# The modulation of layer 2, computed beside layer 1's attention and scan instead of beside its output join

## The chip, the cores and the metric

The kernel runs on one core of a Trainium2 chip. The metric is the device time of one execution in microseconds (us); the median of three runs is compared. The engines of the core run side by side, each through its own list of instructions in a fixed order: PE multiplies matrices, DVE (VectorE) and ACT (ScalarE) do elementwise work and reductions, POOL (GpSimd) does some elementwise work, and SP only issues DMA transfers. An instruction that waits for a semaphore holds up everything behind it on its engine.

## The reference

Two layers on 512 tokens of width 1024, in float32. Layer 1 has a sparse attention branch (8 heads, a top-128 selection of keys) and a state space branch (a chunked scan over 4 groups of heads). Their outputs are joined, projected and added to `x` under a gate. Layer 2 has a band attention, a gated delta rule and a retrieval of experts ("peer"). Both layers are modulated by a vector that depends only on a conditioning vector `c`, and not on any token:

```
mod  = silu(c)   @ ada_w + ada_b        # layer 1: shift, scale, gate     (3 x 1024)
x    = x + gate * (merged @ w_out)      # the gate is needed only here
mod2 = silu(c_2) @ w_ada + b_ada        # layer 2: six parts              (6 x 1024)
```

The last 1024 columns of `mod` and the 6144 of `mod2` are the subject here. Nothing that is computed in between depends on them, so they can be computed at any place before the output projection of layer 1.

## The kernel before

All weights are float32. A weight matrix comes in blocks of 128 x 1024 (512 KB). `wload` (line 50 on) loads a block into a tile `wr`, ACT rounds it to `wh` (L51) and DVE, or POOL in a few places, computes the rest `wl` (L52). `gemm_t` then does 24 matmuls with it (L72 to L74), three per 128 rows, into a PSUM tile `g`. The tiles `wr` form one ring of four buffers in the order of the program: block n+4 can be loaded only after the last reader of block n is done.

The modulation is made of 56 such blocks, 8 for layer 1's gate and 48 for layer 2. A block is loaded into the same ring `wr` (L856), and one DVE instruction (L857) multiplies it by `silu(c)` and sums each row into a column of `acc2`. PE has no part in it. Ahead of the blocks of each layer stand the load of `c` (also a buffer of the ring), a tanh on ACT (L851) and two DVE instructions (L852, L853). After every 8 blocks L860 adds the bias. `mod_rest` makes a list of these 56 steps, and `pump(n)` takes the next n of them at the place where it is called.

Layer 1 runs in this order: the projections and top-k rounds that prepare the attention, with 8 gemms (`ssd_pre`) beside them; 8 attention heads (`att1_head`, each with one gemm of `w_za` and four softmax steps of 128 to 512 keys, `soft`); then for each of four groups the scan (`ssd_scan`), a gate of four gemms (`ssd_z`, weights `w_zs`), and four gemms that prepare the next group (`ssd_x`, `w_x`); then the join `out1`, which reads the attention output (`oatt_d`) and the scan output (`y_d`) back from memory and runs 48 gemms (`w_g`, `w_ba`, `w_bs`, `w_o`).

A softmax step runs through four engines: PE scores (L534), DVE maximum (L545, L547), ACT exponential (L549), DVE reciprocal and scaling (L551, L552), PE transposes (L556), ACT copy, PE product with the values (L560). The order on each engine is set by a scheduler when the program is built: it places the instructions of several steps between each other by its own estimate of their times, but takes buffers of a ring strictly in the order of the program. So gemms of later heads and of `ssd_x` stand between the steps of an attention head on PE. In the kernel before, `mod_rest` is called at the top of `out1`, and the pumps stand among its gemms.

Of the kernel before, what the change touches and what calls it, by code (L numbers as in the profile page):

```python
# [26 lines left out]
class Kernel:  # L27
# [218 lines left out]
    def layer1(self, st0):  # L246
        tc, nc, I = self.tc, self.nc, self.i
        cp = self.cp
        with ExitStack() as st:
            hp = st.enter_context(tc.tile_pool(name="hp", bufs=1, side="right"))  # L250
            mod = cp.tile([P, 24], F32, tag="mod1", name="mod1")
            G1 = cp.tile([P, 8], F32, tag="G1", name="G1")
            hs = [(self.t(hp, [P, T], F32R, f"hh{k}"), self.t(hp, [P, T], F32R, f"hl{k}")) for k in range(8)]
            with ExitStack() as s0:
                p0 = s0.enter_context(tc.tile_pool(name="p0", bufs=1))
                sc = self.silu_c(p0, "c_b")
                acc = p0.tile([P, 16], F32, tag="acc", name="acc1")
                xs = []
                for k in range(8):
                    x = self.t(p0, [P, T], F32, f"x{k}")  # L260
                    nc.sync.dma_start(x, I["xT"][:, k, :])
                    xs.append(x)
                ab = self.load(p0, "ada_b", [P, 24])
                ng = self.load(p0, "norm_g", [P, 8])

                self.ws = []

                def pre(k):
                    if k in (1, 2, 4, 6):
                        k0 = 2 * len(self.ws)  # L270
                        self.ws.append(self.wload(I["w_idx"][:, k0:k0 + 2, :]))
                    self.mod_block(p0, sc, "ada_w", 8 + k, acc)
                    self.mod_block(p0, sc, "ada_w", k, acc)
                    nc.vector.tensor_add(mod[:, k:k + 1], acc[:, k:k + 1], ab[:, k:k + 1])
                    nc.vector.tensor_add(mod[:, 8 + k:9 + k], acc[:, 8 + k:9 + k], ab[:, 8 + k:9 + k])
                    nc.vector.scalar_tensor_tensor(G1[:, k:k + 1], mod[:, 8 + k:9 + k], 1.0, ng[:, k:k + 1],
                                                   op0=OP.add, op1=OP.mult)

                ss = []
                for k in range(8):  # L280
                    sq = self.t(p0, [P, T], F32, "nm_sq", 4)
                    nc.scalar.activation(sq, xs[k], AF.Square)
                    if k not in (0, 6):
                        nc.vector.tensor_add(sq, sq, sp)
                    if k in (5, 7):
                        ss.append(sq)
                    sp = sq
                self.norm_mod(p0, xs, hs, G1, mod[:, 0:8], ss, pre)
            self.mod1 = mod
            self.gate1 = mod[:, 16:24]  # L290
            self.oatt_d = self.dr.tile([8, P, T], F32, tag="oatt_d", name="oatt_d")
            self.y_d = self.dr.tile([16, P, T], F32, tag="y_d", name="y_d")
            with ExitStack() as s1:
                self.ap = s1.enter_context(tc.tile_pool(name="at", bufs=1, reuse_waits="tile"))
                self.sp = s1.enter_context(tc.tile_pool(name="sp", bufs=1, reuse_waits="tile"))
                with tc.tile_pool(name="ap0", bufs=1, side="right", reuse_waits="tile") as self.ap0:
                    self.att1_pre(hs)
                    self.ssd_pre(hs)
                    self.pump(99)
                self.gp = s1.enter_context(tc.tile_pool(name="gp", bufs=1, side="right", reuse_waits="tile"))  # L300
                for h in range(8):
                    self.att1_head(h, hs)
                xs = self.ssd_x(0, hs)
                for g in range(4):
                    y = self.ssd_scan(g, xs)
                    zz = self.ssd_z(g, hs)
                    if g < 3:
                        xs = self.ssd_x(g + 1, hs)
                    self.ssd_gate(g, y, zz)
            self.est = ExitStack()  # L310
            self.ep = self.est.enter_context(tc.tile_pool(name="ep", bufs=1, reuse_waits="tile"))
            with ExitStack() as s2:
                self.out1(s2, hs)
# [360 lines left out]
    def ssd_z(self, g, hs):  # L674

        nc = self.nc
        zs = []
        for b in range(4):
            z = self.gemm_t(self.i["w_zs"][4 * g + b], 8, hs)
            tz = self.t(self.sp, [P, T], F32, "cv_t", 2)  # L680
            nc.scalar.activation(tz, z, AF.Tanh, scale=0.5)
            zz = self.t(self.ap, [P, T], F32, f"qT{b}")
            nc.vector.scalar_tensor_tensor(zz, tz, 1.0, z, op0=OP.add, op1=OP.mult)
            zs.append(zz)
        return zs

    def ssd_scan(self, g, xs):
# [93 lines left out]
    def out1(self, st, hs):  # L781
        tc, nc, I = self.tc, self.nc, self.i
        op = st.enter_context(tc.tile_pool(name="op", bufs=1, reuse_waits="tile"))
        self.mod_rest(op)
        half = []
        ehalf = [self.t(self.ep, [P, 4, T], F32, f"e{j}") for j in range(2)]
        for m in range(8):
            x = ehalf[m // 4][:, m % 4]
            self.gate(m, hs, x)
            half.append(x)  # L790
            self.pump(1 if m else 0)

        def parts(dram, n, tag):
            res = []
            for b in range(n):
                raw = self.t(op, [P, T], F32, "o_raw", 2)
                nc.sync.dma_start(raw, dram[b])
                hi = self.t(op, [P, T], F32R, f"{tag}h{b}")
                lo = self.t(op, [P, T], F32R, f"{tag}l{b}")
                self.split(raw, hi, lo)  # L800
                res.append((hi, lo))
            return res

        oa = parts(self.oatt_d, 8, "p")
        for m in range(8):
            yp = self.gemm_t(I["w_ba"][m], 8, oa)
            nc.vector.scalar_tensor_tensor(half[m], half[m], 1.0, yp, op0=OP.add, op1=OP.mult)
            self.pump(2)
        ys = parts(self.y_d, 16, "ys")
        ms = []  # L810
        for m in range(8):
            mg = self.t(op, [P, T], F32, "o_mg", 2)
            self.gate(8 + m, hs, mg)
            yp = self.gemm_t(I["w_bs"][m], 16, ys)
            nc.vector.scalar_tensor_tensor(mg, mg, 1.0, yp, op0=OP.add, op1=OP.mult)
            nc.vector.tensor_add(mg, mg, half[m])
            self.pump(4)
            hi = self.t(op, [P, T], F32R, f"ph{m}")
            lo = self.t(op, [P, T], F32R, f"pl{m}")
            self.split(mg, hi, lo, scale=0.5)  # L820
            ms.append((hi, lo))
        self.x1_d = self.dr.tile([8, P, T], F32, tag="x1_d", name="x1_d")
        self.x1 = []
        ex = [self.t(self.ep, [P, 4, T], F32, f"e{j}") for j in range(2)]
        for m in range(8):
            x = self.t(op, [P, T], F32, "o_raw", 2)
            nc.sync.dma_start(x, I["xT"][:, m, :])
            ps = self.gemm_t(I["w_o"][m], 8, ms)
            y = ex[m // 4][:, m % 4]
            nc.vector.scalar_tensor_tensor(y, ps, self.gate1[:, m:m + 1], x, op0=OP.mult, op1=OP.add)  # L830
            nc.sync.dma_start(self.x1_d[m], y)
            self.x1.append(y)
            self.sq_add(op, "o_mg", y, m, 8)
# [965 lines left out]
```

## Time and profile before

| | us |
|---|---|
| median of 3 runs (2573.65 to 2576.68) | 2576.07 |
| the profiled execution | 2574.48 |
| its span, from the first to the last instruction | 2572.8 |
| the 8 heads: first score to the last store of `oatt_d` | 198.5 to 331 |
| scan groups | about 345 to 585 |
| join `out1` | about 585 to 850 |

The profile gives the busy time of each engine in a stretch, the groups of instructions, who waited for whom, and the instructions in order of time. PE's busy time is made of pipelined matmuls: a row of 0.39 us starts 0.23 us after the one before it, so the count of matmuls in a stretch says more than its busy time. The granted clock of PE is shown as a share of 2.4 GHz.

### The profile page before, as it was taken

What the parts mean: (1) busy time and instruction counts of PE and PEld (TensorE: products, weight loads), DVE (VectorE), ACT (ScalarE), POOL (GpSimd) and SP (SyncE); (2) the same over time, 40 slices, a digit from 0 to 9 for tenths busy, and PEclk for the clock granted to TensorE, in tenths of its full rate; (3) what the DMA queues carried; (4) which work ended last, traced back from release to release, by engine and by line L of the source; (5) the groups of instructions that cost most, each with busy time, mean ns of one, the idle gap of its engine ahead of it and who ended that gap; (6) DMA issues with size and microseconds to landing.
All of it is one profiled execution on the core that took longest, in us unless ns stands there. A gap on an engine that the chain in (4) does not pass through costs nothing. (4 is left out here: it accounts for less than half of the span.)

```text
span 2572.8 us, 34773 instructions
## 1 busy us (share of the span) xinstructions
PE 2451.5 (95%) x12577; PEld 2043.5 (79%) x12577; DVE 1867.7 (73%) x3618; ACT 1052.5 (41%) x1881; POOL 693.8 (27%) x522
## 2 busy tenths in 40 slices
PE   5999999999999999899998889999899999999999
PEld 4777777778788778776777888999888888888887
DVE  8895666667764673555426899999777878888877
ACT  4444466653322443344433433444433333333332
POOL 3240010110001112420204556211343334443431
PEclk8999999999999999999999999999999999999999
DMA  7222212228865311101422466799999999989995
GB/s 248 75 80 81 74 56 79 69 72 285 288 223 183 110 58 50 58 21 50 137 82 83 145 192 194 270 327 331 334 309 331 335 329 345 355 308 332 337 337 207
DMA packets 199596, 500.43 MB, mean 195 GB/s; under 512 B 20096, under 2 KB 85888, under 8 KB 196352
## 3 DMA queue, kind: packets, MB, share of 16 engines
q1 hardware_dynamic: 159104, 338.81, 39.7%
q0 software_dynamic: 36864, 134.23, 14.7%
q10 hardware_dynamic: 3456, 25.17, 2.4%
q8 instruction: 99, 1.62, 0.3%
q14 instruction: 73, 0.60, 0.1%
HBM read 448.01 MB, written 50.14 MB: 194 GB/s over the span
## 5 line engine op out<-in xcount | busy, mean ns | idle before, releaser
L51 ACT ACTIVATE wh<-wr 128x1024 fp32r<-128x1024 f32 (+2 forms) x424 | 442.6, 1046 | 622.8 <-PE g L73 337.1
L74 PE MATMUL g<-hh,wl 128*128 128x384 f32 (+1 forms) x1792 | 660.2, 368 | 23.8 <-POOL wl L52 20.5
L72 PE MATMUL g<-hh,wh 128*128 128x384 f32 (+1 forms) x1792 | 665.0, 371 | 15.5 <-ACT act L1639 10.0
L73 PE MATMUL g<-hl,wh 128*128 128x384 f32 (+1 forms) x1792 | 659.2, 368 | 0.0
L52 DVE TENSOR_TENSOR wl<-wr,wh 128x1024 fp32r<-128x1024 f32 (+3 forms) x362 | 440.4, 1217 | 189.7 <-ACT wh L51 187.3
L74 PEld LDWEIGHTS g<-hh,wl 128*128 128x128 f32 x1792 | 342.5, 191 | 61.6 <-POOL wl L52 23.5
L72 PEld LDWEIGHTS g<-hh,wh 128*128 128x128 f32 x1792 | 342.4, 191 | 52.8 <-ACT act L1639 10.8
L73 PEld LDWEIGHTS g<-hl,wh 128*128 128x128 f32 x1792 | 342.1, 191 | 38.8 <-issue 8.6
L73 PE MATMUL acc<-wl,gh 128*128 128x512 f32 x768 | 303.8, 396 | 0.0
L74 PE MATMUL acc<-wh,gl 128*128 128x512 f32 x768 | 303.7, 395 | 0.0
L72 PE MATMUL acc<-wh,gh 128*128 128x512 f32 x768 | 303.7, 395 | 0.0
L1676 POOL DMA_INDIRECT row<-in_rows_dn,idx x128 | 167.1, 1306 | 357.0 <-DVE row L1682 315.4
L1676 POOL DMA_INDIRECT row<-in_rows_up,idx x128 | 175.2, 1369 | 268.5 <-DVE gacc L1695 249.0
L52 POOL TENSOR_TENSOR wl<-wr,wh 128x1024 fp32r<-128x1024 f32 x62 | 152.5, 2468 | 239.5 <-ACT wh L51 230.6
L51 ACT ACTIVATE gh<-ga 128x384 fp32r<-128x384 f32 x128 | 67.2, 525 | 335.5 <-issue 193.7
L1682 DVE SCALAR_TENSOR_TENSOR row<-row,h2n 128x1024 f32<-128x1024 f32 x128 | 166.3, 1309 | 21.7 <-DMA row<-in_rows_dn,idx 21.7
L74 PEld LDWEIGHTS acc<-wh,gl 128*128 128x128 f32 x768 | 144.4, 188 | 34.7
L73 PEld LDWEIGHTS acc<-wl,gh 128*128 128x128 f32 x768 | 144.4, 188 | 34.4
L72 PEld LDWEIGHTS acc<-wh,gh 128*128 128x128 f32 x768 | 144.4, 188 | 34.4
L1695 DVE SCALAR_TENSOR_TENSOR gacc<-row,gw,gacc 128x1024 f32<-128x1024 f32 x127 | 162.6, 1280 | 11.8 <-DMA row<-in_rows_up,idx 10.8
L52 DVE TENSOR_TENSOR gl<-ga,gh 128x384 fp32r<-128x384 f32 x128 | 73.3, 572 | 58.7 <-ACT gh L51 50.3
L98 PE MATMUL g<-wh,hh 128*128 128x512 f32 (+3 forms) x256 | 96.1, 377 | 13.4 <-ACT hh L223 11.8
(553 smaller groups left out, 3851.9 us busy)
## 6 DMA issues: line engine op xcount, KB each, us to landing
wr<-in_w_dn SPq DMA_DIRECT2D x128, 512.0 KB
wr<-in_w_up SPq DMA_DIRECT2D x128, 512.0 KB
wr<-in_ada_w SPq DMA_DIRECT2D x56, 512.0 KB
g_d<-stage ACTq DMA_DIRECT2D x24, 1024.0 KB
gr<-g_d SPq DMA_DIRECT2D x32, 768.0 KB
wr<-in_w_x SPq DMA_DIRECT2D x24, 512.0 KB
act_d<-act SPq DMA_DIRECT2D x63, 192.0 KB
ar<-act_d SPq DMA_DIRECT2D x63, 192.0 KB
```

What stands on the lines that cost most here:

```text
L51: nc.scalar.activation(hi, src, AF.Copy)
L52: eng.tensor_sub(lo, src, hi.bitcast(F32))
L72: mm(ps, ah, bh, start=first, stop=False)
L73: mm(ps, ah, bl, start=False, stop=False)
L74: self.mm = mm(ps, al, bh, start=False, stop=last)
L98: mm(pss[t], hh[:, tt], wh[:, k], start=f, stop=False)
L1676: nc.gpsimd.indirect_dma_start(r, None, src, bass.IndirectOffsetOnAxis(ap=self.idx[:, s:s + 1], axis=0))
L1682: nc.vector.scalar_tensor_tensor(r, r, 1.0, self.h2n, op0=OP.mult, op1=OP.mult, accum_out=act[:, s:s + 1])
L1695: nc.vector.scalar_tensor_tensor(acc, r, w[:, s:s + 1], acc, op0=OP.mult, op1=OP.add)
```

## The change

The call of `mod_rest` moves from the top of `out1` to the place ahead of the loop over the attention heads. The tile for `silu(c)` and the biases move with it into the pool `gp`. The pumps in `out1` go. Instead, 4 blocks are taken after each head (32), and 1, 2, 1 and 2 blocks after the four gemms of each `ssd_z` (24): all 56. In the kernel before, 55 were taken in `out1` and one in the first stage of layer 2.

```
@@ layer1
                 self.gp = s1.enter_context(tc.tile_pool(name="gp", ...))
+                self.mod_rest(self.gp)
                 for h in range(8):
                     self.att1_head(h, hs)
+                    self.pump(4)
@@ ssd_z
             zs.append(zz)
+            self.pump(2 if b % 2 else 1)
@@ out1
         op = st.enter_context(tc.tile_pool(name="op", ...))
-        self.mod_rest(op)
...
             half.append(x)
-            self.pump(1 if m else 0)
...
             nc.vector.scalar_tensor_tensor(half[m], half[m], 1.0, yp, op0=OP.add, op1=OP.mult)
-            self.pump(2)
...
             nc.vector.tensor_add(mg, mg, half[m])
-            self.pump(4)
```

On SP, the list of transfers at the start of the heads was, before, the eight blocks of `w_za` one behind the other, and the blocks of `w_x` right behind them:

```order
L65 DMA wr_1757<-in_w_za 128x1024
L65 DMA wr_1876<-in_w_za 128x1024
L65 DMA wr_1995<-in_w_za 128x1024
L65 DMA wr_2114<-in_w_za 128x1024
L65 DMA wr_2233<-in_w_za 128x1024
L65 DMA wr_2352<-in_w_za 128x1024
L65 DMA wr_2471<-in_w_za 128x1024
L65 DMA wr_2590<-in_w_za 128x1024
L65 DMA wr_2709<-in_w_x 128x1024
L65 DMA wr_2749<-in_w_x 128x1024
```

Now, at the same place of SP's list, four blocks of the modulation stand between one block of `w_za` and the next (line numbers in the changed kernel are a little different: L855 is the L856 of before, L848 the L849):

```order
L65 DMA wr_1763<-in_w_za 128x1024
L848 DMA wr_1881<-in_c_b 128x1024
L855 DMA wr_1887<-in_ada_w 128x1024
L855 DMA wr_1890<-in_ada_w 128x1024
L855 DMA wr_1893<-in_ada_w 128x1024
L44 DMA c_ada_b<-in_ada_b 128x24
L44 DMA c_ada_b_1760<-in_ada_b 128x48
L855 DMA wr_1896<-in_ada_w 128x1024
L65 DMA wr_1900<-in_w_za 128x1024
L855 DMA wr_2018<-in_ada_w 128x1024
L855 DMA wr_2021<-in_ada_w 128x1024
L855 DMA wr_2024<-in_ada_w 128x1024
```

In the ring of four, the second block of `w_za` is now the sixth behind the first, and the first block of `w_x` comes after all 32 blocks of the heads.

On DVE, the stretch from the first maximum of head 0 (128 keys) to that of its second step (256 keys) was, before:

```order
L545 ISA pr_1794,mx_1795<-a_1792,mask_85_354 128x128
L545 ISA mx_1795 128x1
L52 TENSOR_TENSOR wl_2116<-wr_2114,wh_2115 128x1024
L576 SCALAR_TENSOR_TENSOR bc_386_1743<-cv_t_1749,cv_u_1744 128x512
L528 SCALAR_TENSOR_TENSOR zz_1789<-tz_1787,g_1756 128x512
L547 TENSOR_SCALAR nm_1797<-mx_1795 128x1
L551 RECIPROCAL rc_1801<-sm_1799 128x1
L552 TENSOR_SCALAR pr_1794<-pr_1794,rc_1801 128x128
L545 ISA pr_1811,mx_1812<-a_1809,mask_86_355 128x256
```

The same stretch of DVE now (L547, L549, L553, L554 are the L545, L547, L551, L552 of before; L856 is the L857 of a modulation block):

```order
L547 ISA pr_1800,mx_1801<-a_1798,mask_85_354 128x128
L547 ISA mx_1801 128x1
L856 SCALAR_TENSOR_TENSOR wr_1890,acc_1757<-wr_1890,sc_430_1883 128x1024
L549 TENSOR_SCALAR nm_1803<-mx_1801 128x1
L856 SCALAR_TENSOR_TENSOR wr_1893,acc_1757<-wr_1893,sc_430_1883 128x1024
L553 RECIPROCAL rc_1807<-sm_1805 128x1
L856 SCALAR_TENSOR_TENSOR wr_1896,acc_1757<-wr_1896,sc_430_1883 128x1024
L554 TENSOR_SCALAR pr_1800<-pr_1800,rc_1807 128x128
L52 TENSOR_TENSOR wl_1902<-wr_1900,wh_1901 128x1024
L856 SCALAR_TENSOR_TENSOR wr_2018,acc_1757<-wr_2018,sc_430_1883 128x1024
L856 SCALAR_TENSOR_TENSOR wr_2021,acc_1757<-wr_2021,sc_430_1883 128x1024
L547 ISA pr_1817,mx_1818<-a_1815,mask_86_355 128x256
```

Five blocks now stand inside one softmax step, and the only split of weights in it (L52) is that of the second `w_za` block, where before those of the second and third were already behind and that of the fourth stood here.

## Rows read from the trace of the kernel before

**Rows 1.** The page, busy time of each engine over the span:
```profile
PE 2451.5 (95%) x12577; PEld 2043.5 (79%) x12577; DVE 1867.7 (73%) x3618; ACT 1052.5 (41%) x1881; POOL 693.8 (27%) x522
```

**Rows 2.** Busy time by stretch; the last columns: granted clock, DMA share, GB/s:
```profile
194.80:241.70 46.90, 46.06 (x222) 35.16 (x221) 27.04 (x70) 22.14 (x51) 0.07 (x1) 0.98 0.28 90
200.00:345.00 145.00, 141.70 (x720) 106.43 (x719) 84.77 (x222) 72.85 (x171) 10.57 (x5) 1.00 0.23 73
345.00:585.00 240.00, 236.44 (x1180) 172.83 (x1179) 161.44 (x229) 139.19 (x328) 27.23 (x23) 1.00 0.23 74
585.00:650.00 65.00, 65.00 (x283) 52.78 (x282) 49.59 (x72) 22.43 (x28) 0.00 (x0) 1.00 0.87 293
660.00:700.00 40.00, 36.87 (x142) 27.66 (x142) 27.77 (x41) 16.54 (x24) 0.00 (x0) 0.91 0.86 294
700.00:720.00 20.00, 20.00 (x88) 16.17 (x87) 14.60 (x21) 4.45 (x6) 0.00 (x0) 1.00 0.76 239
```

**Rows 3.** DVE in order of time, ends of the stretch of three heads:
```profile
194.80 0.74 DVE L573 SCALAR_TENSOR_TENSOR cv_u<-g,c_conv_w,cv_u 128x509 f32<-128x509 f32 x1
...
241.70 0.56 DVE L545 CUSTOM_DVE_ANT_0 pr<-a,mask 128x384 f32<-128x384 f32 x1 [1.24 <-PE a L534]
```

**Rows 4.** DVE in order of time, modulation steps in the join:
```profile
586.88 0.69 DVE L852 TENSOR_SCALAR sc<-sc 128x1024 f32<-128x1024 f32 x1 [3.67 <-ACT sc L851]
587.61 1.23 DVE L853 TENSOR_TENSOR sc<-sc,wr 128x1024 f32<-128x1024 f32 x1
588.87 1.23 DVE L857 SCALAR_TENSOR_TENSOR wr<-wr,sc 128x1024 f32<-128x1024 f32 x1
...
590.02 1.22 DVE L857 SCALAR_TENSOR_TENSOR wr<-wr,sc 128x1024 f32<-128x1024 f32 x1
```

**Rows 5.** DVE groups of 194.8 to 241.7 that wait, widths apart:
```profile
L551 DVE RECIPROCAL rc<-sm 128x1 f32<-128x1 f32 x10 | 1.6, 161 | 4.9 <-ACT pr L549 4.9
...
L545 DVE CUSTOM_DVE_ANT_0 pr<-a,mask 128x512 f32<-128x512 f32 x2 | 1.4, 692 | 3.1 <-PE a L534 3.1
...
L545 DVE CUSTOM_DVE_ANT_0 pr<-a,mask 128x256 f32<-128x256 f32 x3 | 1.3, 425 | 3.9 <-PE a L534 3.9
L545 DVE CUSTOM_DVE_ANT_0 pr<-a,mask 128x384 f32<-128x384 f32 x2 | 1.1, 554 | 1.2 <-PE a L534 1.2
...
L545 DVE CUSTOM_DVE_ANT_0 pr<-a,mask 128x128 f32<-128x128 f32 x3 | 0.9, 288 | 2.0 <-PE a L534 2.0
```

**Rows 6.** PE in order of time: matmuls at full clock, after a wait, one softmax step:
```profile
187.04 0.40 PE L73 MATMUL g<-hl,wh 128*128 128x512 f32 x1
190.77 0.80 PE L74 MATMUL g<-hh,wl 128*128 128x512 f32 x1 [3.34 <-DVE wl L52]
...
191.79 0.63 PE L73 MATMUL g<-hl,wh 128*128 128x512 f32 x1
192.22 0.63 PE L74 MATMUL g<-hh,wl 128*128 128x512 f32 x1
...
196.43 0.40 PE L72 MATMUL g<-hh,wh 128*128 128x512 f32 x1
196.66 0.39 PE L73 MATMUL g<-hl,wh 128*128 128x512 f32 x1
...
228.43 1.02 PE L534 MATMUL a<-kT,qT 128*128 128x512 f32 x2
229.29 0.88 PE L560 MATMUL a<-pts,v 128*128 128x128 f32 x6
...
232.08 0.60 PE L556 MATMUL a<-ident,pr 128*128 128x128 f32 x4
232.52 0.39 PE L534 MATMUL a<-kT,qT 128*128 128x128 f32 x2
```

**Rows 7.** The modulation's DVE group over the join, and what it waited for:
```profile
L857 DVE SCALAR_TENSOR_TENSOR wr<-wr,sc x56: 1215/1224/1228, 588.9 to 848.4; 128x1024 f32<-128x1024 f32 x56
...
  DMA wr<-in_ada_w: 40.5, 25
```

**Rows 8.** Waits, 655 to 700: total us, times, longest us:
```profile
ACT ysh L51 <- DMA o_raw<-y_d: 23.2, 11, 4.9
...
PE g L73 <- DVE ysl L52: 1.6, 3, 0.7
PE g L72 <- ACT ysh L51: 1.5, 2, 0.8
```

**Rows 9.** DVE at the end of the join, around the last block:
```profile
837.63 0.75 DVE L830 SCALAR_TENSOR_TENSOR e<-g,mod,o_raw 128x512 f32<-128x512 f32 x1 [3.52 <-PE g L74]
...
843.23 0.75 DVE L830 SCALAR_TENSOR_TENSOR e<-g,mod,o_raw 128x512 f32<-128x512 f32 x1 [4.23 <-PE g L74]
...
848.35 1.23 DVE L857 SCALAR_TENSOR_TENSOR wr<-wr,sc 128x1024 f32<-128x1024 f32 x1 [3.75 <-DMA wr<-in_ada_w]
...
849.50 0.75 DVE L830 SCALAR_TENSOR_TENSOR e<-g,mod,o_raw 128x512 f32<-128x512 f32 x1
```

More of the change, by code (lines that the diff above doesn't have):

```diff
@@ L300, in layer1 @@
                 self.gp = s1.enter_context(tc.tile_pool(name="gp", bufs=1, side="right", reuse_waits="tile"))
+                self.mod_rest(self.gp)
                 for h in range(8):
                     self.att1_head(h, hs)
+                    self.pump(4)
                 xs = self.ssd_x(0, hs)
@@ L684, in ssd_z @@
             zs.append(zz)
+            self.pump(2 if b % 2 else 1)
         return zs
@@ L783, in out1 @@
         op = st.enter_context(tc.tile_pool(name="op", bufs=1, reuse_waits="tile"))
-        self.mod_rest(op)
         half = []
@@ L790, in out1 @@
             half.append(x)
-            self.pump(1 if m else 0)
         def parts(dram, n, tag):
@@ L807, in out1 @@
             nc.vector.scalar_tensor_tensor(half[m], half[m], 1.0, yp, op0=OP.add, op1=OP.mult)
-            self.pump(2)
         ys = parts(self.y_d, 16, "ys")
@@ L816, in out1 @@
             nc.vector.tensor_add(mg, mg, half[m])
-            self.pump(4)
             hi = self.t(op, [P, T], F32R, f"ph{m}")
```

## The prediction

> **What bounds the kernel now.** I read the page's busy times first, then a table by stretch, then the stretches in order of time. PE is busy 95% of the span [rows 1], and the reader is to see in the table that it is so in each stage that the change touches: 141.7 of 145 us in the heads, 236.4 of 240 in the scan groups, all of 65 us in the first part of the join [rows 2]. The modulation costs PE nothing, so its 56 instructions can only show in the time where they keep a weight block or a softmax step from PE. Before, there is one place of that kind. A stretch of 20 us of plain gemms holds 88 matmuls (700 to 720); 660 to 700 holds 142 instead of 176, with the transfers at 294 GB/s [rows 2]. There ACT waits 23.2 us for the read-back of `y_d`, and PE waits for the tiles made from it [rows 8]; the blocks of the modulation share the transfers of that stretch.
>
> **The join, which is rid of 55 blocks.** The 34 matmuls missing in 660 to 700, at 0.23 us from one to the next (196.43 to 196.66) [rows 6], are 7.8 us. Without the blocks the read-back has the transfers nearly to itself, so I take 7.5 us as won; the bounds are 0 (the read-back is slow by itself) and 7.8. DVE is idle for about a quarter of the join (49.6 of 65 us busy) [rows 2], so the DVE time that goes is worth nothing there. One more block stands at the end of the join: its instruction at 848.35 waited 3.75 us for its transfer and is done 1.15 us later, and the last sum (L830) follows at 849.50. The two sums before it are 5.6 us apart (837.63, 843.23), so it was due at about 848.8 [rows 9]: 0.7 us. Together the join gives 8.2 us, and nothing more can be had: the rest of it runs at 88 matmuls in 20 us.
>
> **The heads, which take 32 blocks.** The price of a block on DVE is the distance of two of them, 588.87 to 590.02, so 1.15 us; L852 and L853 with the wait between them are 2.0 us for each `c` [rows 4]. All 56 have nearly the same duration, 1.22 us [rows 7]. Where the blocks stand is decided by the new order of DVE. I compared the stretch from the last of the top-k masks to the maximum over 384 keys of the third head. Before and after hold the same 70 DVE instructions, with 7 splits of weights; the new one has 31 blocks, two pairs L852 and L853 and three sums L860 (0.3 us) between them. Before, the stretch lasted from 194.8 to 241.7, 46.9 us [rows 3], with DVE busy for 27.0 [rows 2]. Now DVE needs 27.0 + 31 x 1.15 + 2 x 2.0 + 0.3 = 67 us for it: the third head is at least 20 us late there. Part of that is not lost, since PE does more other work meanwhile. Counted in its new order, 158 weight matmuls stand between the first score and that third head's score, before 120; 38 x 0.23 = 8.7 us. So PE is behind by 20.1 - 8.7 = 11.4 us if DVE never waits. If DVE keeps all of its 19.9 us of idle time in the stretch beside the blocks, it is 31.3 us. Those are the bounds. Of the idle time, the waits for ACT (4.9 us at L551) are now covered by a block that stands ahead of each reciprocal; the waits for scores from PE, 3.1 + 3.9 + 1.2 + 2.0 = 10.2 us [rows 5], are covered only in part, since PE in turn waits for the splits and softmax steps. I keep 7 of them: 18.4 us.
>
> The transfers point the same way. 41 blocks of 0.524 MB (32 and two `c`, seven of `w_za`) must pass the ring in that stretch, 21.5 MB. At the 293 GB/s that the join reached with a DMA share of 0.87 [rows 2] they take 73 us, which is the 67 with some 6 of waiting. The Trainium skill, page "DMA: Bandwidth & Descriptors", section "Where 436 GB/s comes from", puts the memory limit of a core at about 358 GB/s; as an estimate by that page 60 us would do, the transfers would add no wait, and the sum would come out nearer its lower bound; no stretch in rows 2 shows such a rate.
>
> Behind the stretch, PE's new order has two softmax steps with no weight matmul between (from the third head's 512 keys on), because the blocks of `w_x` stand behind all 32 in the ring. A step from 512 keys to the next score takes 4.1 us (228.43 to 232.52), of which PE's own score, value product and transposes are 2.5 [rows 6]; two of them leave PE idle for about 3 us. After that PE has the same work and fillers as before and does not catch up, because it was already full there. The heads cost 18.4 + 3 = 21.4 us.
>
> **The scan groups, which take 24 blocks.** DVE is busy 161.4 of 240 us there [rows 2]; 24 x 1.15 = 27.6 us fit in the 78.6 idle. Bounds: 0, if all lie in gaps, and 27.6, if each lies on the chain of the scan. A gain is excluded, since nothing leaves this stage. PE has so many gemms between the scan's steps that it idles 3.6 us in 240, so I stay near the lower end: 2 us.
>
> **Sum.** Against the profiled execution, 2574.5 us: + 21.4 + 2 - 8.2 = 2589.7. The median of the runs is 1.6 us above that execution, so 2591 on its scale. The case's own range: lower end 11.4 + 0 - 8.2, so 2579; upper end 31.3 + 3 + 5 - 4, so about 2611.
>
> **The rivals.**
> *The blocks fit into the gaps, faster.* DVE idles 60 us of 145 in the heads and 78.6 of 240 in the scan groups [rows 2], against 41 and 28 us added, and the heads move only 73 GB/s where the join moves 293. If the lag of the third head stays under 8.7 + 8.2 = 16.9 us, only the gain of the join is left; with all hidden it is 2576 - 8 = 2568. Against it: 31 blocks stand beside less than three of the eight heads, where 19.9 us are idle and not 60, and 20.1 is the least lag. It decides from a stretch of under 64 us. The Trainium skill, "Perfetto Trace Analysis", section "Optimization Strategy", says that stages with different busiest engines can gain from being interleaved; that rule leads to this case, and on averages the trace agrees (DMA share 0.23 against 0.87).
> *The clock falls, slower still.* After PE's wait of 3.34 us at 187 to 190.8, matmuls came 0.43 us apart instead of 0.23, at 1.2 instead of 2.4 GHz, until about 196; 12 of them, 2.4 us lost [rows 6]. In the new stretch PE has 46.1 + 8.7 = 55 us of work in 67 to 74 us, so it waits in several places, one of them about 7 us long (the first transposes of head 0 stand behind four blocks). If the clock stays low for most of the stretch, its matmuls cost up to 158 x 0.2 = 32 us more, of which the 12 to 19 us of waiting absorb a part: 15 to 20 us on top, about 2608. For it: the fall at 190 came after a single wait. Against: while PE waits for DVE, a slow matmul costs only where DVE waits for its score.
> *The join gives nothing back.* The stall at 660 to 700 waits for `y_d`, 16 loads through two buffers, and not for the blocks [rows 8]; if it stays, the 7.5 us go: 2598. Against: the new order on SP reads `y_d` two at a time beside `w_ba`, which is earlier.
> That the change doesn't do what it says is excluded: in the new order all 56 blocks stand ahead of the first block of `w_g`.
>
> **Chances.** The forecast's case 0.62, the gaps 0.13, the clock 0.10, the join without gain 0.15. The measurement tells 0.2%, about 5 us, from no change. Slower by more than that: 0.62 less the 0.12 of it that end under 2581, plus 0.25, so 0.75; within 0.2%: 0.12; faster: 0.13. The range from 2573 to 2615 leaves out the gaps' case and a part of the clock's.
>
> **What would show it.** Right: from 195 to about 267 DVE is busy nearly throughout, PE has waits for L52 and L552 there, and the maximum over 384 keys of the third head comes 20 to 30 us later than 241.7; the last store of `oatt_d` comes later than 331; the 40 us that hold the read-back of `y_d` have over 170 matmuls; the scan groups take 240 us and a few more. Wrong: that score is less than 17 us late, or PE has more weight matmuls in between than 158, then the heads are free; or the join holds the same 142 matmuls; or the scan groups grow by over 10 us, then DVE stood on the scan's chain and I undercounted.

## The result and the profile after

The changed kernel takes 2603.98 us (median of 4 runs, 2599.24 to 2608.55) against 2574.95 us of the kernel before, run beside it: a ratio of 1.0114, with a 95% interval of 1.0101 to 1.0126. It is slower, by some 29 us; the forecast was 2591, with a range of 2573 to 2615. The profiled executions are 24.7 us apart (spans of 2597.5 and 2572.8 us). The busy times in the page of the kernel after are the old ones [rows 1], so the loss is waiting:

```profile
PE 2452.6 (94%) x12577; PEld 2050.5 (79%) x12577; DVE 1867.6 (72%) x3618; ACT 1052.5 (41%) x1881; POOL 700.4 (27%) x522
```

Busy time by stretch in the kernel after, in the columns of [rows 2] (PE, PEld, DVE, ACT, POOL with their instructions, then granted clock, DMA share, GB/s). The first row is the stretch of three heads at its new length, the second the 51 us behind it:

```profile
194.80:268.80 74.00, 59.38 (x258) 44.25 (x257) 64.10 (x139) 24.81 (x53) 0.00 (x0) 0.91 0.80 273
268.80:320.00 51.20, 41.39 (x190) 31.39 (x191) 30.73 (x80) 20.74 (x45) 9.50 (x4) 0.87 0.42 139
345.00:585.00 240.00, 233.06 (x1165) 170.91 (x1163) 174.53 (x282) 145.91 (x359) 29.64 (x19) 0.99 0.32 106
420.00:440.00 20.00, 15.43 (x67) 11.92 (x67) 11.66 (x18) 7.90 (x23) 5.83 (x4) 0.83 0.46 157
660.00:700.00 40.00, 40.00 (x179) 33.13 (x177) 22.30 (x28) 15.50 (x20) 0.00 (x0) 1.00 0.62 196
700.00:720.00 20.00, 20.00 (x89) 16.46 (x88) 7.47 (x8) 5.36 (x6) 0.00 (x0) 1.00 0.26 81
```

The stretch is 74.0 us long where it was 46.9, with DVE busy 64.1 of them. The join has no hole: 179 matmuls in 660 to 700, 142 before.

Three marks on DVE, in order of time, cut the difference: the maximum over 384 keys of the third head, the last gate of the scan (L774, the L771 of before), and the last two sums of layer 1 (L829, the L830 of before):

```profile
268.80 0.56 DVE L547 CUSTOM_DVE_ANT_0 pr<-a,mask 128x384 f32<-128x384 f32 x1 [0.17 <-PE a L536]
...
619.11 1.41 DVE L774 SCALAR_TENSOR_TENSOR y<-y,c_ssm_norm_g,a 128x512 f32<-128x512 f32 x2
...
870.02 0.75 DVE L829 SCALAR_TENSOR_TENSOR e<-g,mod,o_raw 128x512 f32<-128x512 f32 x1 [4.07 <-PE g L74]
875.47 0.75 DVE L829 SCALAR_TENSOR_TENSOR e<-g,mod,o_raw 128x512 f32<-128x512 f32 x1 [4.07 <-PE g L74]
```

Before, the last gate of the scan was here:

```profile
580.49 0.75 DVE L771 SCALAR_TENSOR_TENSOR y<-y,c_ssm_norm_g,a 128x512 f32<-128x512 f32 x1
```

So the kernel after is 27.1 us late at the third head [rows 3], 38.6 us at the end of the scan, and 26.0 us at the last sum [rows 9]. The join took 269.0 us from gate to last sum (580.49 to 849.50) and takes 256.4 (619.11 to 875.47): it gives back 12.6, where I had 8.2.

Comparing the times at which PE starts its n-th matmul in the two traces, the kernel after is behind by 33.8 us at 330 us of before, 34.0 at 350, 31.5 at 380, 41.3 at 410, and 38.6 from 585 to 620. So the heads cost 34, and the scan some 5 more, in one place.

One thing about the blocks themselves: the scheduler didn't keep the 24 blocks of the scan behind the heads. In DVE's order, 40 of the 56 blocks (L856) stand ahead of the last head's last score (369.3), and not 32: eight of the scan's 24 are beside the later heads.

What PE waits for, in order of time (idle time and releaser in brackets):

```profile
206.07 0.80 PE L72 MATMUL g<-hh,wh 128*128 128x512 f32 x1 [8.39 <-ACT wh L51]
...
277.40 1.12 PE L558 MATMUL a<-ident,pr 128*128 128x128 f32 x4 [3.26 <-DVE pr L554]
...
297.96 1.11 PE L558 MATMUL a<-ident,pr 128*128 128x128 f32 x4 [3.68 <-DVE pr L554]
...
425.03 1.22 PE L112 MATMUL a<-ones,gsqa 128*128 128x1 f32 x5 [4.57 <-POOL gsqa L204]
```

The first wait is in the stretch. The two at L558 are behind it: transposes that wait for their own softmax step, with no weight matmul to do. With two of 0.3 us, PE waits 7.6 us for transposes' inputs from 268.8 to 320. The last is at the gate of the first scan group, for a sum of squares on POOL.

In the join, the read-back of `y_d` is ready nearly when ACT wants it (waits of 620 to 700: total, times, longest; before 23.2 us, [rows 8]):

```profile
ACT ysh L51 <- DMA o_raw<-y_d: 4.1, 7, 1.0
```

### The profile page after: what moved, and what is told of

Its sections match the earlier page's. It is cut to its first block, busy times and chain, and to the rows that moved or that the text cites. A ratio compares the mean times of both kernels' runs of the same rounds, so it can differ in the third digit from the quotient of the medians.

```text
span 2597.5 us, 34741 instructions
## 1 busy us (share of the span) xinstructions
PE 2452.6 (94%) x12577; PEld 2050.5 (79%) x12577; DVE 1867.6 (72%) x3618; ACT 1052.5 (41%) x1881; POOL 700.4 (27%) x522
## 3 DMA queue, kind: packets, MB, share of 16 engines
q0 software_dynamic: 36864, 134.23, 14.6%
## 5 line engine op out<-in xcount | busy, mean ns | idle before, releaser
L52 DVE TENSOR_TENSOR wl<-wr,wh 128x1024 fp32r<-128x1024 f32 (+3 forms) x362 | 443.5, 1226 | 239.5 <-ACT wh L51 237.2
L52 POOL TENSOR_TENSOR wl<-wr,wh 128x1024 fp32r<-128x1024 f32 x62 | 152.5, 2470 | 259.7 <-ACT wh L51 258.6
L1681 DVE SCALAR_TENSOR_TENSOR row<-row,h2n 128x1024 f32<-128x1024 f32 x128 | 172.1, 1354 | 23.9 <-DMA row<-in_rows_dn,idx 23.9
L52 DVE TENSOR_TENSOR gl<-ga,gh 128x384 fp32r<-128x384 f32 x128 | 73.3, 573 | 57.7 <-ACT gh L51 57.6
```

What stands on the lines that cost most here:

```text
L52: eng.tensor_sub(lo, src, hi.bitcast(F32))
L1681: nc.vector.scalar_tensor_tensor(r, r, 1.0, self.h2n, op0=OP.mult, op1=OP.mult, accum_out=act[:, s:s + 1])
```

## The experiments

Theory 1: the price is DVE's time in its fixed order, blocks between softmax steps. Theory 2: the shared ring, in which weights stand behind blocks. Theory 3: the bytes. For the join there are an address theory (A) and one of contention (B). In each run of the kernel before beside them its median was 2575.6 to 2576.9.

### e1_after_shift32

In the join of the kernel after, two sums are 5.45 us apart (5.44 on average over the last four), 5.60 before [rows 9], though in neither kernel a block stands beside these gemms. The only other difference is where the tiles lie: `mod_rest(op)` had put 4384 bytes first into the pool.

```
+        pad = self.t(op, [P, 8], F32, "pad")
+        nc.vector.memset(pad, 0.0)
```

> The kernel after, with 32 unused bytes per partition put first in the join's pool: its tiles ph, pl, ysh and ysl lie at byte addresses that are multiples of 64 again, as in the kernel before (in the kernel after they lie 32 bytes beside such a multiple). Nothing else moves. Theory A (the address sets the pace): the join's matmuls come 0.2333 us apart instead of 0.2267, as before; 768 of them x 6.7 ns = 5.1 us, so about 2609 against 2604 of the kernel after. Theory B (the blocks of the modulation slowed the matmuls, and they are gone): 0.2267 us stays and the time is 2604.

Measured: 2610.07 us (2605.68 to 2612.29). On DVE the last gate of the scan is at 621.14; the last two sums:

```profile
876.40 0.75 DVE L831 SCALAR_TENSOR_TENSOR e<-g,mod,o_raw 128x512 f32<-128x512 f32 x1 [4.24 <-PE g L74]
881.99 0.75 DVE L831 SCALAR_TENSOR_TENSOR e<-g,mod,o_raw 128x512 f32<-128x512 f32 x1 [4.23 <-PE g L74]
```

5.59 us again: A holds. The join is 881.99 - 621.14 = 260.9 us here, 8.2 less than before. That is what the blocks had cost there, the forecast's number; the other 4.5 us came from the addresses.

### e2_before_shift32

The same two lines in the kernel before.

> The kernel before, with the same 32 bytes first in the join's pool, so that ph, pl, ysh and ysl lie 32 bytes beside a multiple of 64. All blocks of the modulation stay in the join. Theory A (the address): matmuls of the join 0.2267 us apart, the last sums of the join 5.44 instead of 5.60 us apart, about 5 us less: 2570 against 2575. Theory B (the blocks beside them): 0.2333 us and 2575 stay.

Measured: 2574.3 us, ratio 0.9998 (0.9989 to 1.0007). The last undisturbed sums, 5.49 us apart:

```profile
834.95 0.75 DVE L832 SCALAR_TENSOR_TENSOR e<-g,mod,o_raw 128x512 f32<-128x512 f32 x1 [3.41 <-PE g L74]
840.44 0.75 DVE L832 SCALAR_TENSOR_TENSOR e<-g,mod,o_raw 128x512 f32<-128x512 f32 x1 [4.13 <-PE g L74]
```

The join is 2.5 us shorter (266.5), half of the expected gain and not to be told from none in the total. 32 beside a multiple of 64 is not the whole rule: here the tiles lie at 96 mod 128, in the kernel after at 32.

### e3_own_ring

```
+                with tc.tile_pool(name="hb", ...) as self.hb:
                     for h in range(8): ...
-            w = self.t(self.wp, [P, 1024], F32, "wr", 4)
+            w = self.t(self.hb, [P, 1024], F32, "mw", 3) if self.hb else self.t(self.wp, ..., "wr", 4)
```

> The kernel after, with the 32 blocks of the heads (and the two c) in three buffers of their own; the four buffers of weight blocks hold weights alone, so the loads of w_za and w_x no longer stand behind modulation blocks. The blocks stand on DVE between the same softmax steps. Theory 1 (DVE's time in order is the price): the third head's 384 maximum still comes 20 us or more late, and the total falls by 5 us at most, 2599 to 2605. Theory 2 (the shared ring is the price: weights come late, and PE has no gemm to do beside softmax steps): PE finds w_x gemms behind the stretch, the 15 us lost there go, and part of the stretch too: 2575 to 2590.

Measured: 2603.88 us. The third head's maximum comes 2.9 us earlier than in the kernel after; then PE runs dry, with the clock at 0.70 (PE had 85 and 91 matmuls in the two slices before):

```profile
265.93 0.56 DVE L551 CUSTOM_DVE_ANT_0 pr<-a,mask 128x384 f32<-128x384 f32 x1 [1.20 <-PE a L540]
```
```profile
240.00:260.00 20.00, 13.09 (x49) 9.68 (x49) 15.02 (x38) 5.20 (x12) 2.65 (x1) 0.70 0.75 249
```

Theory 2 falls. With weights at hand early, PE does its gemms early and lacks them later; the softmax steps come no faster. (27 blocks stand ahead of that maximum here, 31 in the kernel after, since the scheduler made a new order.)

### e4_short_mul

```
-            nc.vector.scalar_tensor_tensor(w, w, 1.0, cur[cname], ...)
+            q = slice(0, 128)
+            nc.vector.scalar_tensor_tensor(w[:, q], w[:, q], 1.0, cur[cname][:, q], ...)
```

> The kernel after, where the multiply and sum of a modulation block goes over 128 of its 1024 columns (the rest of the product is left out); all transfers and the ring stay. Theory 1 (DVE's time is the price): 31 blocks x about 0.95 us = 29 us less DVE time in the stretch, and the heads lose 25 us or more of their 34: 2572 to 2582. Theory 3 (the transfers are the price: 21.5 MB at 293 GB/s need 73 us whatever DVE does): the stretch stays at 65 to 75 us, and the total is 2595 to 2605.

Measured: 2578.4 us, 26 less than the kernel after. A block takes 0.28 us, and the third head is 2.9 us late instead of 27.1:

```profile
230.97 0.28 DVE L857 SCALAR_TENSOR_TENSOR wr<-wr,sc 128x128 f32<-128x128 f32 x1
...
244.64 0.56 DVE L547 CUSTOM_DVE_ANT_0 pr<-a,mask 128x384 f32<-128x384 f32 x1 [1.03 <-PE a L536]
```

Theory 1 holds in the total. Two reserves. The order is planned from the durations, and 20 blocks, not 31, stand ahead of that maximum here. And the third head's time flatters: PE has done 85 weight matmuls ahead of that score, where the kernel before had done 120, so by the count of matmuls PE is 10.8 us behind there, and 12.3 at 330 us of before. The end of the scan is at 597.20, still 16.7 late. What is left with the short multiplies, 12.3 of the 33.8 us of the heads, has all the transfers in it.

### e5_paced

```
+        self.last = nc.vector.tensor_scalar(pr, pr, rc, None, op0=OP.mult)
...
+                with self.tc.issue_after(self.last.ins):
+                    nc.vector.scalar_tensor_tensor(w, w, 1.0, cur[cname], ...)
```

> The kernel after with the 32 blocks of the heads in three buffers of their own (as in e3_own_ring), and each block put on DVE right behind one softmax step (one per step, four per head) in place of 31 before the third head's 384 maximum. Same work on every engine. Theory 1a (it is the place in DVE's order that costs: 31 blocks beside less than three heads): ahead of that maximum stand 10 blocks instead of 31, four blocks a head need 4.6 us of the 7.5 us that DVE idles per head, the maximum comes within 10 us of the 241.7 of the kernel before, and most of the 34 us go: 2570 to 2585. Theory 1b (the blocks cost their DVE time wherever they stand among the heads: 32 x 1.15 + 4 = 41 us): 2595 to 2610.

Measured: 2591.47 us (2586.67 to 2599.69), between the two ranges. The third head is nearly in time (4.2 us late), and PE does 274 matmuls at full clock in 200 to 260 (286 before). The loss comes at the end of the heads:

```profile
245.90 0.56 DVE L552 CUSTOM_DVE_ANT_0 pr<-a,mask 128x384 f32<-128x384 f32 x1
```
```profile
200.00:260.00 60.00, 55.24 (x274) 41.45 (x273) 48.45 (x116) 25.45 (x55) 4.96 (x2) 1.00 0.71 229
...
320.00:340.00 20.00, 14.24 (x64) 9.55 (x63) 13.17 (x37) 6.30 (x16) 0.00 (x0) 0.84 0.54 167
340.00:360.00 20.00, 14.72 (x64) 11.22 (x62) 14.99 (x32) 12.73 (x34) 0.00 (x0) 0.73 0.04 14
```

At the end of the scan it is 31.1 us late (611.62). In PE's order, 4 matmuls on weights stand between the seventh head's score over 512 keys and the last head's over 384, and none from there to that over 512; the kernel before has 26 and 12. So the place in the order moves the loss and does not remove it; 1b is nearer. My reading of these counts: a block behind each step makes each step longer, PE spends more gemms per step, and they are gone in the last two heads.

### e6_scan_join

The blocks of the scan stay; those of the heads go to the join, with a new `silu(c)` there.

```
-                    self.pump(4)
...
+        self.mod_pool(op)
...
+            self.pump(4)    # beside w_bs
```

> No block beside the heads: 24 go beside the scan as in the kernel after, the other 32 into the join, four beside each block of w_bs, behind the loads of y_d; the join's tiles stay 32 bytes beside a multiple of 128. Theory (heads, scan and join add up as the traces have them): the third head's 384 maximum comes at 241 to 243, the scan groups cost 2 to 8 us, the stall of the kernel before at 660 to 700 is gone (7.5 us), and the addresses give 5: about 2568 (2563 to 2573). Rival (the blocks in the join stall it wherever they stand): 20 us slices below 85 matmuls come back beside w_bs and the time is 2576 or more.

Measured: 2581.25 us, 1.0012 of before (1.0002 to 1.0022): missed by 13. DVE, the end of the scan and the last sums:

```profile
592.89 2.72 DVE L773 SCALAR_TENSOR_TENSOR y<-y,c_ssm_norm_g,a 128x512 f32<-128x512 f32 x4 [1.09 <-PE a L136]
...
852.19 0.75 DVE L831 SCALAR_TENSOR_TENSOR e<-g,mod,o_raw 128x512 f32<-128x512 f32 x1 [4.20 <-PE g L74]
857.77 0.75 DVE L831 SCALAR_TENSOR_TENSOR e<-g,mod,o_raw 128x512 f32<-128x512 f32 x1 [4.21 <-PE g L74]
```

The 24 blocks alone cost 12.4 us; the scheduler put 9 of them ahead of the last head's last score (346.6). The join gains 4.1 us only; no stall is left in 620 to 740, but the sums are 5.58 apart, with the tiles at 32 mod 256, and the three slices from 760 to 820 hold 85, 82 and 86 matmuls. So the rival's sign is there too, in small.

### e7_short_load

```
-            nc.sync.dma_start(w, self.i[wname][b])
+            nc.sync.dma_start(w[:, :128], self.i[wname][b][:, :128])
-            nc.vector.scalar_tensor_tensor(w, w, 1.0, cur[cname], ...)
+            nc.vector.scalar_tensor_tensor(w, cur[cname], 1.0, cur[cname], ...)
```

> The kernel after, where each modulation block is loaded in 128 of its 1024 columns only, and the multiply takes the silu of c for both operands at full width (the modulation is left out, DVE's time for it stays). Theory 1 (DVE's time in order): the third head's 384 maximum stays at 262 to 270, the total at 2590 to 2605. Theory 3 (the 21.5 MB of transfers): the maximum moves back to 242 to 250, the total to 2570 to 2582.

Measured: 2589.94 us, 14 less than the kernel after, at the edge of theory 1's range.

```profile
263.42 0.56 DVE L547 CUSTOM_DVE_ANT_0 pr<-a,mask 128x384 f32<-128x384 f32 x1 [1.75 <-PE a L536]
```
```profile
280.00:300.00 20.00, 18.18 (x88) 13.39 (x87) 11.17 (x34) 7.91 (x19) 2.37 (x1) 0.97 0.22 68
```

The stretch stays long with an eighth of the modulation's bytes (DVE is busy 64.9 of its 68.6 us): DVE sets it. Of the rest, transfers are a part: the third head gains 5.4 us, the end of the heads 8.7 by the count of matmuls (25.1 us behind at 330 of before, 33.8 in the kernel after), the end of the scan (607.80) 11.3. The slice from 280 to 300 holds 88 matmuls (62 in the kernel after), but the steps stand elsewhere in it: from the third head to 320 it is 224 in 56.6 us here, and 190 in 51.2 there. The order was planned anew here too: 32 blocks stand ahead of the maximum.

### e8_hp_shift64

```
+            nc.vector.memset(self.t(hp, [P, 16], F32, "pad"), 0.0)
```

> The kernel after, with 64 unused bytes in the pool of the normed input of layer 1, so that its tiles hh and hl lie at 32 mod 128, as the weights wh and wl do, instead of 96 mod 128. Theory A (the offset of the moving operand mod 128 sets the pace: 0.2267 us at 32, 0.2286 at 96, 0.2333 at 0 or 64): the matmuls on hh and hl come 0.2267 us apart, some 2,800 of them x 1.9 ns = 5 us, about 2599 where PE is the bound throughout, less gain where it is not. Rival: the 0.2286 belongs to the stage and not to the address; 2604 stays.

Measured: 2603.31 us. The pace changes (PE, a gate's matmuls: 23 steps from 702.42 to 707.64, 0.2270 us), the total does not: 0.7 us is inside the spread of the runs (2599.93 to 2607.14). That PE waits for others in most of the stages that use these tiles would explain it; no run shows it.

### e9_before_late

```
+        nc.vector.memset(self.t(op, [P, 56], F32, "pad"), 0.0)
-            self.pump(1 if m else 0)
+            self.pump(1)
-            self.pump(2)                      # beside w_ba
+            self.pump(3 if m < 5 else 1)      # beside w_o
```

> The kernel before (all blocks in the join), with three edits in the join: no block beside w_ba, where y_d is read back, and the 16 of them beside w_o instead; the first block one w_g earlier; 224 unused bytes first in the pool, so that ph, pl, ysh and ysl lie at 160 mod 256, as the weights do (in e6_scan_join they lay at 32 mod 256 and the sums came 5.57 us apart, not 5.44). Theory (what the join gave back in the kernel after needs no block to leave it): the stall at 660 to 700 goes, 7.5 us; matmuls at 0.2267 us, 5.1 us; sum 12.6, so about 2564 against 2576. Rival (the transfers of the blocks stall the join at any place): one of the two stays, 2569 to 2571, or a stall comes in the w_o stage.

Measured: 2585.11 us, slower than before: 1.0038 (1.0024 to 1.0052). My theory fell. The stall at 660 to 700 is gone and the sums are 5.44 apart, but a new stall stands at the start of w_o. PE in order of time, and DVE ahead of it:

```profile
817.78 0.80 PE L72 MATMUL g<-ph,wh 128*128 128x512 f32 x1 [8.97 <-ACT ph L54]
```
```profile
810.61 1.23 DVE L858 SCALAR_TENSOR_TENSOR wr<-wr,sc 128x1024 f32<-128x1024 f32 x1 [0.97 <-DMA wr<-in_ada_w]
...
813.49 1.23 DVE L858 SCALAR_TENSOR_TENSOR wr<-wr,sc 128x1024 f32<-128x1024 f32 x1 [1.65 <-DMA wr<-in_ada_w]
...
816.38 0.69 DVE L816 TENSOR_TENSOR o_mg<-o_mg,e 128x512 f32<-128x512 f32 x1
```

Blocks stand on DVE ahead of the last merge of w_bs (L816) and wait there for their transfers, and the merge behind them waits with them; ACT's `ph` needs the merge, and PE needs `ph`. In 740 to 830 DVE waited 31.4 us for blocks, 17 times. There is a second, smaller loss: 585 to 605 holds 60 matmuls at a granted clock of 0.83 (89 at 1.00 before), and PE is 6.8 us behind at 620. It stands where the first block was brought one w_g forward; no run tells that edit from the others.

### e10_all_shift

e9_before_late with the line of e8_hp_shift64 in the pools of `hh` and `hl` of both layers and of the last stage.

> e9_before_late with 64 unused bytes in three more pools, so that hh and hl of both layers and of the last stage, and with them gh and gl, lie at 160 mod 256 as the weights do. Theory (PE is the bound of layer 1 in this order, so a shorter matmul pays there, as it could not in e8_hp_shift64 where DVE was the bound): some 2,800 matmuls x 1.6 ns = 4.5 us in layer 1, and up to 10 us more in layer 2 and the last stage: 2552 to 2560. Rival (as e8_hp_shift64: the pace changes, the time does not): 2562 to 2566.

Measured: 2576.2 us (2565.78 to 2582.1), 9 less than e9_before_late. Layer 1 is not shorter (last sum at 860.26, there 859.59); the last stage holds more matmuls in the same time, first here, then e9_before_late:

```profile
1950.00:2570.00 620.00, 618.85 (x2909) 534.89 (x2907) 512.38 (x624) 219.89 (x301) 239.13 (x173) 1.00 0.93 330
```
```profile
1950.00:2570.00 620.00, 620.00 (x2857) 525.44 (x2855) 502.60 (x608) 218.43 (x298) 233.71 (x171) 1.00 0.92 325
```

So the address pays, but not in the layer for which I had worked it out. Both ranges missed, since both had taken 2564 for e9_before_late. The 9 us are a balance: by the count of matmuls, this run wins 14.4 us on e9_before_late from matmul 8,000 to the last, and loses 10.1 between matmuls 4,500 and 6,000, in layer 2; why it loses there is open.

### e11_heads_join

Built as e6_scan_join, with `self.pump(4)` back after each head, none in `ssd_z`, and 3 beside each block of w_bs.

> The 32 blocks of the heads stay as in the kernel after (shared buffers, the same order up to the third head); the 24 of the scan go into the join, three beside each block of w_bs, behind the loads of y_d; ph at 160 mod 256. The scan is free of blocks. Theory (terms add up): heads +34, scan 0, join -13: 2597, against 2604 with the scan's +7. Rival (the scan's loss is carried over from the heads, not made by its blocks): the stretch of the scan still loses 5 us or more and the time is 2602 or more.

Measured: 2593.96 us (2590.55 to 2597.68); theory 2597. The end of the scan and the last sum:

```profile
614.84 2.72 DVE L773 SCALAR_TENSOR_TENSOR y<-y,c_ssm_norm_g,a 128x512 f32<-128x512 f32 x4 [0.93 <-PE a L136]
...
871.18 0.75 DVE L831 SCALAR_TENSOR_TENSOR e<-g,mod,o_raw 128x512 f32<-128x512 f32 x1 [4.08 <-PE g L74]
```

34.4 us late at the end of the scan without a block in it. By PE's counts the heads are about 30 of these (31.4 at 330 us of before, 30.6 at 380), and 3.0 follow at the first gate (75 matmuls in 400 to 420, clock 0.83). So a stall at the first gate comes without any block beside the scan. But it is smaller than that of the kernel after (9.8 us from 380 to 410 of before, of which 2.7 come back). PE's waits for POOL there, in us, times, longest, 350 to 640, of the kernel after, of this run and of e6_scan_join, which has no block of the heads:

```profile
PE a L112 <- POOL gsqa L204: 6.4, 2, 4.6
PE a L112 <- POOL gsqa L204: 2.1, 2, 1.3
PE a L112 <- POOL gsqa L204: 4.5, 2, 2.7
```

In e5_paced, with blocks in both places, it is 1.8 us. So neither group of blocks is its cause alone, and it does not go with the lag of the heads (34, 31, 7 and 30 us at 330 us of before in these four); the cause stays open. The rival's time did not come either.

### e12_half_heads

As e11_heads_join, with 2 after each head and 5 beside each block of w_bs.

> As e11_heads_join with 16 blocks in the heads instead of 32 (two per head in the code; all 16 stand ahead of the third head's 384 maximum) and 40 in the join. Theory L (the price goes with the number of blocks): half of 34, 17 us, third head at about 255: 2576 + 17 - 13 = 2580. Theory G (DVE's idle time takes a first part for nothing): DVE needs 27 + 16 x 1.15 + 2 x 2 + 0.2 = 49.6 us in the stretch of 46.9, 2.7 us more plus 7 of its waits, less the gemms that PE does meanwhile: third head at 245 to 252, heads +2 to +8, about 2568.

Measured: 2578.8 us, 1.0017 of before (1.0008 to 1.0026).

```profile
257.08 0.56 DVE L547 CUSTOM_DVE_ANT_0 pr<-a,mask 128x384 f32<-128x384 f32 x1 [1.18 <-PE a L536]
...
595.10 2.72 DVE L773 SCALAR_TENSOR_TENSOR y<-y,c_ssm_norm_g,a 128x512 f32<-128x512 f32 x4
...
851.85 0.75 DVE L831 SCALAR_TENSOR_TENSOR e<-g,mod,o_raw 128x512 f32<-128x512 f32 x1 [4.08 <-PE g L74]
```

16 blocks cost 14.6 us, 32 cost 34.4 (e11_heads_join): 0.91 and 1.08 us each. Theory L is much nearer than G: the third head is 15.4 us late and the time is 2579, where G had 3 to 10 and 2568. Whether a first few microseconds are free, these two runs can't tell: the profiled execution of this one took 2576.57 us, 2.2 less than the median, and that of the other 2597.68, 3.7 more. The join is 256.8 us long with 40 blocks in it, as short as with none; none of them stands beside the read-back of `y_d`.

## Why the prediction was right or wrong, point by point

**What bounds the kernel.** Right. PE is full in every stage touched [rows 2], its busy time is the same in both kernels, and the loss is mostly time in which it waits.

**The stretch of three heads, 18.4 us.** Right in that DVE sets it, and right in size: 27.1 us late with 36 more matmuls done (258 against 222), 8.3 us, so 18.8; the 158 weight matmuls ahead of the third head's score are those that I had counted. In two of its terms the size is luck. DVE was busy 64.1 us where I had 67, and waited 74.0 - 64.1 = 9.9 us where I had kept 7; the two errors of 2.9 us cancel. And the 7 us were to be waits for scores from PE. The trace has 2.7 us of these in 194.8 to 268.8; most of the others hang on transfers (DVE's waits: total, times, longest):

```profile
DVE wl L52 <- ACT wh L51: 4.3, 4, 1.6
DVE pr L547 <- PE a L536: 2.7, 3, 1.7
DVE wr L856 <- DMA wr<-in_ada_w: 1.8, 3, 0.8
DVE rc L553 <- ACT pr L551: 0.7, 1, 0.7
```

That DVE sets the stretch is shown by e7_short_load, and in the main by e4_short_mul. The line on transfers (73 us at 293 GB/s) was no second proof: with an eighth of the modulation's bytes the stretch is still 68.6 us, though the rest of the bytes is worth 5.4 us of it (the first and third of these waits are 0.5 us and none there). One sign did not come: PE's waits for L52 are only 1.7 us in the stretch and it has none for the scaled scores; its long wait, 8.39 us, is for ACT's `wh` of the second `w_za` block. With that wait gone (e3_own_ring) the time stayed.

**Behind the stretch, 3 us.** This is the step that failed. The prediction said that two softmax steps would lack filler, and that "after that PE has the same work and fillers as before and does not catch up". From 268.8 to 320 the kernel after does 190 matmuls in 51.2 us with PE busy 41.4. The heads cost 33.8 in all, so 15 behind the stretch. Two parts of it are seen in rows: 9.8 us of waiting, of which transposes wait 7.6 for their softmax step where I had 3, and a granted clock of 0.87, which can't have cost more than (1 - 0.87) x 51.2 = 6.7 us, an estimate from the row. e7_short_load shows that the transfers are in it: the heads end 8.7 us earlier there, 3.3 of them won after the third head. Eight blocks that I had put down to the scan are in it too; e11_heads_join, without them, has about 30 at the end of the heads, but it doesn't separate them from the spread of the runs. The explanation that fits e12_half_heads and e5_paced, argued and not tested by itself, is this: a softmax step takes its time on DVE one instruction behind the other, PE has a limited store of gemms to cover them, and most of what is put into the steps is owed at the end. At 1.15 us a block and 2 us for each `c`, 16 blocks put 22 us into DVE's order and cost 14.6, and 32 put 41 into it and cost 34.4. I had counted idle time and fillers of three heads only.

**The scan, 2 us.** The size at the end was 4.8 (38.6 less 33.8), and it is not 24 blocks spread over the scan's gaps: eight stood beside the heads, and the loss is at one place, the first gate, where 3 us come with blocks in the heads alone (e11_heads_join). What the 24 blocks add to the other 32 lies between the 4 us by which the traces of the kernel after and e11_heads_join differ at the end of the scan, and the 10 us between their medians. Alone, with the heads undisturbed, they cost 12.4 (e6_scan_join), where nine of them were placed beside the heads.

**The join, -8.2 us.** Right in what it named: e1_after_shift32, with the addresses of before, gains 8.2. The prediction had no term for another 4.5 us, which came because the tiles of `silu(c)` and the biases left the pool and all tiles behind them moved.

**Sum.** 18.8 + 15.0 + 4.8 - 12.6 = 26.0, the lag at the last sum; the forecast had 18.4 + 3 + 2 - 8.2 = 15.2. The medians are 29 us apart; the profiled execution of the kernel after took 2599.24, 4.7 less than its median, so some 3 us of the 29 are in no trace. That 2604 lies inside the forecast's range is luck in part: the room above 2591 was meant for waits inside the stretch, which came out as forecast, while the term behind it had 3 us at most.

**The rivals.** *The gaps hold the blocks* fell: even 16 blocks cost 14.6 us, and one block per step, with the scan's 24, 31. The time that DVE idles in the heads lies inside the chain score, maximum, exponential, product, and a block put there is added to the chain. The rule that the prediction named beside it (the Trainium skill, "Perfetto Trace Analysis", "Optimization Strategy") speaks of stretches with different most-contended engines, which may gain from being interleaved. By busy time PE was the busiest in both places, 141.7 of 145 us and 65 of 65 [rows 2]; the DMA shares of 0.23 and 0.87, in which the prediction saw the trace agree, don't show that the condition is met. So these runs don't refute the rule. *The clock falls* came true in its sign and not in its size: 0.74 in 200 to 220 and 0.84 in 280 to 300 of the kernel after. Over 194.8 to 268.8 and 268.8 to 320 the clock can have cost (1 - 0.91) x 74.0 + (1 - 0.87) x 51.2 = 13.3 us at most, an estimate that counts PE's waits as work, so the 15 to 20 us of this rival are excluded there, though its 2608 is nearer to the time measured than my 2591. How much less than 13.3 it was is not shown. In e5_paced the clock was 1.00 up to 260, and the heads still lost. *The join gives nothing back* fell by e1_after_shift32.

No run was faster than the kernel before. One that leaves the heads free and gives the join the blocks as e12_half_heads does was not tried; its two halves were measured apart only (e9_before_late with undisturbed heads, e12_half_heads with 256.8 us for the join).

## What to carry to other kernels

Idle time of an engine inside a chain of dependent steps is not free room: an instruction put there lengthens the chain, and if the engine that waits for it has a limited store of other work, the debt comes due where the store runs out, even if the first steps look undisturbed. So sum the chain over the whole stage against the whole store, not over the stretch where most of the new work stands, and look in the planned order for where each piece really lands. Where a tile is moved out of a pool, look at where the tiles behind it land.

## What the runs showed of the hardware

The pace of a matmul of 512 columns depends on where the two operands lie in the memory of the core. With weights at 160 mod 256 and the other operand at 160, 224, 32 and 192 mod 256, matmuls came 0.2267 (the kernel after, 5.44 us for 24), 0.2288 (e2_before_shift32, 5.49), 0.2325 (e6_scan_join, 5.58) and 0.2333 us apart (before, 5.60). In the last stage, where the roles are exchanged, moving `gh` and `gl` from 224 to 160 brought it from 0.233 us (e9_before_late, nine steps from 2199.87 to 2201.97) to 0.227. PE in e10_all_shift, `gl`, `gh` and again `gl`:

```profile
2199.72 0.39 PE L74 MATMUL acc<-wh,gl 128*128 128x512 f32 x1
2199.94 0.39 PE L72 MATMUL acc<-wh,gh 128*128 128x512 f32 x1
...
2201.98 0.39 PE L72 MATMUL acc<-wh,gh 128*128 128x512 f32 x1
```

Nine steps from 2199.94 to 2201.98 are 2.04 us. The addresses are those that the build gave the tiles. A pair at 160 and 224 took 0.2288 us in the join and 0.233 in the last stage, so the role counts too. Equal offsets were the fastest in each case; why, and whether the offset itself or the difference matters, the runs don't tell.
